# One inversion over nine chunks of a head pair, where two ran over four and five

## The chip, the core and the metric

The program runs on one core of a Trainium2 chip. A core has a matrix engine (PE, whose weight loads are listed as PEld), three elementwise engines (DVE, ACT, POOL) and a queue that issues DMAs (SP). Each engine runs its own list of instructions strictly in the order in which they stand, and waits on semaphores for the others. The metric is the time of one execution on the device in microseconds; the profile is one such execution, taken by the hardware profiler.

## The reference, cut to what matters

Two decoder layers over 512 tokens and 16 learned ones in front (528 in all, width 1024): an RWKV-7 time mixing layer (32 heads of 64), then a latent attention layer. The change lies in the first. Its core is a recurrence over the tokens, one 64x64 state a head:

```python
def step(S, inp):
    r_t, w_t, k_t, v_t, a_t, b_t = inp
    sa = jnp.einsum('bhij,bhj->bhi', S, a_t)
    S = S * w_t[:, :, None, :] + sa[..., None] * b_t[:, :, None, :] + v_t[..., None] * k_t[:, :, None, :]
    return S, jnp.einsum('bhij,bhj->bhi', S, r_t)
```

The term `sa` makes each token depend on all before it in its chunk. Taken 64 tokens at a time, that dependence is a unit triangular 64x64 system for each chunk and head, and its inverse can be made before the state is known.

## The kernel before, in words

Tokens are cut into nine chunks of 64 (the last holds 16). Heads go in pairs, `p` from 0 to 15: one head on partitions 0 to 63, the other on 64 to 127. For each pair the program

- projects k and r (`multiply`: 96 matmuls `pg<-x,w` of 264 columns), and normalises and decays them (`prepare`);
- makes the triangular matrices of the nine chunks (`products`: `M`, in three slices: chunks 0 to 3, 4 to 7, 8);
- inverts them (`inverse`): `Mh` is M in f16, `Mb` and `Qb` are block diagonal forms of it, `Lb` is what f16 lost. Five levels (`lv`) double the size of the inverted blocks. In a level PE multiplies by `Mb`, DVE masks the result into `Xs`, ACT copies `Xs` into a padded tile (`X0`, `X1`, `o`), PE multiplies by `Qb` and ACT writes `Tm`; beside this PE and ACT bring `Qb` up to the next level. A correction step then ends with `Qd`, the inverse that the recurrence reads;
- transposes and scales what the state update needs (`sides`: `KBt`, `SV`);
- runs the recurrence (`recur`, `chunk`): per chunk `pc<-SV,ALR`, evacuated as `xs`; `pc<-xs,Qd`, evacuated into `SV`; `pc<-SV,KBt`, which gives the next state; and two matmuls into `py` for the output. Lane 0 takes chunks 0 to 3 of a pair and lane 1 chunks 4 to 8, so that lane 0 can be in the next pair while lane 1 finishes this one;
- normalises the output (`finish`), and much later gates it (`gate`).

Before, the inversion has two lanes too: `inverse(p, 0)` on chunks 0 to 3 and `inverse(p, 1)` on 4 to 8, each a generator of its own that goes through the pairs in order. `CUT = 4` is the border. The tiles of the inversion exist once each, so a lane starts on the next pair when it is done with this one. `M` exists once, `KB` once, `Qd`, `SV` and `KBt` twice, `ALR` and `MR` three times.

What isn't in this chain fills PE between its steps: the projections of the next pairs, and after pair 15's the 16 units of the gate projection g (48 matmuls each, also `<-x,w`), which nothing needs before the recurrence's end. Then come the output projection (`<-y,w`) and the second layer.

The order of all instructions on all engines is decided while the program is built, by a planner (`Flow`). Each stage is a generator that yields steps; the planner keeps a clock for each engine, takes the step that can start first by its own table of costs, and issues it. A stage named earlier in the list wins if it is within `SLACK` microseconds; the wide matmuls of the projections are put back by `DEFER`; where PE would stand idle and has had little work, it adds a matmul on constants (`pc<-masks`). A projection's result goes to two banks `pg`, or, every other time for some kinds, to `pw`, of which there are four for everything else.

Of the kernel before, what the change touches and what calls it, by code (L numbers as in the profile page):

```python
# [130 lines left out]
class Flow:  # L131
# [9 lines left out]
    SLACK, DEFER = 0.1, 0.1  # L141
# [316 lines left out]
class Layer0:  # L458
# [516 lines left out]
    def invert(self, lane):  # L975

        flow = self.flow
        if lane == 0:
            yield from self.blocks()
            for n in ("Tm", "Mh", "Q"):  # L980
                setattr(self, n, self.tl(1, (128, 9, 64), n, F16))
            for t in (self.Tm, self.Mh, self.Q):
                flow.cut[t.tensor.name] = CUT * 64
            for t in (self.Mb, self.Qb, self.Lb, *self.X):
                flow.cut[t.tensor.name] = CUT * 128
            flow.cut[self.Xs.tensor.name] = CUT * 32
            flow.events.add("blocks")
        yield flow.until("blocks")
# [83 lines left out]
    def inverse(self, p, lane):  # L1072
# [5 lines left out]
        Mb, Qb, Lb, Mh, Tm, Q = (t[:, c0:c1] for t in (self.Mb, self.Qb, self.Lb, self.Mh, self.Tm, self.Q))  # L1078
# [25 lines left out]
        q, v = product(lambda ci: I, Mb)  # L1104
        nc.vector.tensor_tensor(Tm, v, bc(self.mL[0], nn), ALU.mult)
        nc.last(q)
        yield
        for lv in range(1, 6):
            b = 1 << lv
            x = self.Xs[:, c0:c1]  # L1110
            x4 = x.rearrange("p c (g b) -> p c g b", b=b)
            m = half(self.mL[lv], b, 0)
            q, v = product(lambda ci: half(Tm[:, ci, :], b, 0), Mb, n=32)
            nc.vector.tensor_tensor(x4, v.rearrange("p c (g b) -> p c g b", b=b),
                                    m.unsqueeze(1).to_broadcast([128, nn, 32 // b, b]), ALU.mult)
# [6 lines left out]
            q, v = product(lambda ci: x[:, ci, :], Qb, n=32)  # L1122
# [12 lines left out]
        q, v = product(lambda ci: Tm[:, ci, :], Mb, Lb)  # L1135
# [3 lines left out]
        for hs in (H0, H1):  # L1139
            nc.vector.tensor_tensor(Eb[hs, :, hs], bc(self.id16[hs], nn), v[hs], ALU.subtract)  # L1140
        nc.last(q)
        yield
        q, v = product(lambda ci: I, Tb)
        nc.scalar.activation(Q, v, AF.Copy)
        nc.last(q)
# [118 lines left out]
    def stages(self):  # L1264
# [3 lines left out]
        return [self.finish(), self.recur(1), self.recur(0), self.sides(), self.invert(0), self.invert(1), self.within(), self.prepare(), self.tables(), self.norm(),  # L1268
# [932 lines left out]
```

## Time and profile before

| | |
|---|---|
| median of three executions | 1610.45 us (1608.45 to 1613.81) |
| the profiled execution | 1609.79 us, of which the span of its instructions is 1608.0 us |
| PE, DVE, ACT, POOL busy | 1463.8, 1034.9, 942.4, 733.9 us |
| projections of v, lerps, decays | 0 to about 212 us |
| the pairs, from the first inversion to the end of the recurrence | 212.6 to 934.4 us |
| rest of g, output projection of layer 0 | to about 1080 us |
| layer 1 | to 1608 us |

Times in the rows are microseconds from the start of the span, busy times are sums over instructions, and a wait is put down to what came last. A busy PE isn't a PE at its peak: matmuls overlap, and an alone standing small one counts with its whole latency.

### The profile page before, as it was taken

Reading aid. Unit: us, or ns where it says so; the run is one execution under the profiler, and the core shown is the slowest. Engines: PE = TensorE matmul, PEld = TensorE weight load, DVE = VectorE, ACT = ScalarE, POOL = GpSimd, SP = SyncE. Lnnn points to the kernel's source line nnn. Section 1 sums busy time; section 2 is a strip of 40 time slices with the busy share of each in tenths; the row PEclk is TensorE's granted clock in tenths of the full one; section 3 lists DMA queues with packets and bytes.
Section 4 is the critical chain, followed back from the end, with each engine's and each line's share of the span. In section 5 each row is a group of like instructions: output and inputs, shape, how many; then the busy total and the mean of one; then the engine's idle time right before and its main releaser. Section 6 shows DMA issues by size and latency. Waiting matters only on the chain. (4 is left out here: it accounts for less than half of the span.)

```text
span 1608.0 us, 33360 instructions
## 1 busy us (share of the span) xinstructions
PE 1463.8 (91%) x12404; PEld 1301.2 (81%) x12404; DVE 1034.9 (64%) x2304; ACT 942.4 (59%) x2467; POOL 733.9 (46%) x877
## 2 busy tenths in 40 slices
PE   3899988899998998999998999999999999989997
PEld 3898877888887887888887899998778778877786
DVE  7995688787788877778777333035476666656503
ACT  3556655767766667677777674445555545544532
POOL 4453555444544435444445565745523222322654
PEclk7999999999999999999999999999999999999998
DMA  3456622122122122112422257533211111211332
GB/s 113 133 188 223 205 81 74 43 68 68 55 64 66 61 68 68 49 61 88 143 74 82 69 164 253 171 101 93 82 46 48 53 46 54 53 51 45 112 94 84
DMA packets 84690, 148.49 MB, mean 92 GB/s; under 512 B 9392, under 2 KB 18480, under 8 KB 84528
## 3 DMA queue, kind: packets, MB, share of 16 engines
q1 hardware_dynamic: 84528, 146.37, 28.9%
q8 instruction: 97, 1.59, 0.4%
q14 instruction: 65, 0.53, 0.1%
HBM read 112.87 MB, written 33.46 MB: 91 GB/s over the span
## 5 line engine op out<-in xcount | busy, mean ns | idle before, releaser
L322 POOL TENSOR_TENSOR w<-wraw,w 128x512 fp32r<-128x512 f32 (+1 forms) x278 | 371.6, 1343 | 478.8 <-ACT w L322 448.6
L322 PE MATMUL pg<-x,w 128*128 128x264 f32 x2064 | 337.5, 299 | 7.7 <-ACT k L322 3.2
L322 PEld LDWEIGHTS pg<-x,w 128*128 128x128 f32 x2064 | 272.7, 189 | 13.7 <-ACT k L322 5.7
L322 ACT ACTIVATE w<-wraw 128x512 fp32r<-128x512 f32 (+1 forms) x278 | 170.2, 615 | 135.7 <-DMA wraw<-wo 58.5
L322 POOL COPY Sd<-SV 64x64 f32<-64x64 f32 x256 | 73.1, 286 | 187.9 <-DVE SV L322 180.3
L322 PE MATMUL pb<-u,w 128*128 128x512 f32 x384 | 106.2, 405 | 11.9 <-DVE sg L322 11.9
L322 PE MATMUL pg<-lat,w 128*128 128x512 f32 (+1 forms) x480 | 108.5, 367 | 4.9 <-DVE q L322 3.1
L322 PEld LDWEIGHTS pg<-lat,w 128*128 128x128 f32 x480 | 80.6, 197 | 17.4 <-DVE q L322 3.5
L322 PEld LDWEIGHTS pb<-u,w 128*128 128x128 f32 x384 | 68.4, 190 | 25.8 <-DVE sg L322 14.2
L322 PE MATMUL pg<-O,w 128*128 128x512 f32 x336 | 79.1, 395 | 3.2 <-ACT acc L322 1.5
L322 PEld LDWEIGHTS pg<-O,w 128*128 128x128 f32 x336 | 62.9, 188 | 19.1 <-ACT acc L322 1.9
L322 DVE SCALAR_TENSOR_TENSOR SV<-Sd,PC,pc 64x64 f32<-64x64 f32 x224 | 59.8, 279 | 22.3 <-PE pc L322 17.5
L322 PE MATMUL pc<-xs,Qd 128*128 128x64 f32 x288 | 54.4, 286 | 20.4 <-ACT xs L322 19.0
L322 PEld LDWEIGHTS <-Mb 128*128 128x128 f16 x1152 | 59.0, 98 | 16.4 <-issue 6.4
L322 POOL TENSOR_TENSOR Lb<-M,Mh 64x256 f16<-64x256 f32 (+1 forms) x64 | 50.4, 787 | 42.8 <-ACT Mh L322 38.8
L322 PEld LDWEIGHTS pc<-xs,Qd 128*128 128x128 f32 x288 | 41.4, 189 | 34.3 <-ACT xs L322 29.8
L322 PE MATMUL pc<-SV,KBt 128*128 128x128 f32 x256 | 54.2, 312 | 9.5 <-DVE SV L322 7.6
L322 DVE SCALAR_TENSOR_TENSOR sg<-sg,par,rs 128x264 f32<-128x264 f32 x32 | 16.0, 532 | 71.9 <-ACT rs L322 71.9
L322 DVE TENSOR_TENSOR Xs<-pw,masks 128x128 f16<-128x128 f32 (+1 forms) x160 | 47.7, 301 | 21.4 <-PE pw L322 9.6
L322 DVE COPY SV<-pc 64x64 f32<-64x64 f32 x176 | 36.3, 225 | 38.4 <-ACT SV L322 32.7
L322 PE MATMUL pw<-Tm,Mb 128*128 128x32 f16 (+1 forms) x864 | 54.7, 180 | 4.8 <-ACT Tm L322 3.8
L322 PE MATMUL pc<-SV,ALR 128*128 128x128 f32 x288 | 57.2, 286 | 1.1 <-ACT xs L322 0.5
(375 smaller groups left out, 3906.7 us busy)
## 6 DMA issues: line engine op xcount, KB each, us to landing
wraw<-wr SPq DMA_DIRECT2D x120, 256.0 KB, 2.9
wraw<-wo SPq DMA_DIRECT2D x64, 256.0 KB, 2.7
wraw<-wi SPq DMA_DIRECT2D x46, 256.0 KB, 2.7
d_v<-gx SPq DMA_DIRECT2D x16, 264.0 KB, 3.0
d_c<-o SPq DMA_DIRECT2D x16, 264.0 KB, 2.4
c<-d_c SPq DMA_DIRECT2D x16, 264.0 KB, 3.0
a<-d_a SPq DMA_DIRECT2D x16, 264.0 KB, 3.1
vx<-d_v SPq DMA_DIRECT2D x16, 264.0 KB, 2.9
```

The costliest lines, as they stand in the source:

```text
L322: getattr(eng, method)(*args, **kw)
```

## The change

`inverse` works on all nine chunks at once, and one generator goes through the pairs. An elementwise operation that stood twice (4 and 5 chunks) stands once over nine; where a product has 64 columns a chunk, nine don't fit a PSUM bank (576 over 512), so it takes two banks, and its evacuation stays two instructions. The inversion of a pair starts on the event that all nine chunks' `M` are there (`("M", p, True)`). The last evacuation into `Qd` keeps its two parts and two waits. `SLACK` goes from 0.1 to 0.12, `DEFER` from 0.1 to 0.05.

```diff
-    SLACK, DEFER = 0.1, 0.1
+    SLACK, DEFER = 0.12, 0.05
...
-    def invert(self, lane):
+    def invert(self):
...
         for p in range(NP):
-            yield flow.until(("M", p, lane == 1))
-            yield from self.inverse(p, lane)
+            yield flow.until(("M", p, True))
+            yield from self.inverse(p)
...
-        c0, c1 = ((0, CUT), (CUT, 9))[lane]
-        nn = c1 - c0
-        M = self.st[p]["M"][:, c0:c1]
+        nn = 9
+        M = self.st[p]["M"]
...
         def product(rhs, *lhs, n=64):
 
-            q = self.one()
-            qv = q[:, 0 : nn * n].rearrange("p (c t) -> p c t", t=n)
-            for ci in range(nn):
-                for i, l in enumerate(lhs):
-                    nc.tensor.matmul(qv[:, ci, :], l[:, ci, :], rhs(ci), start=(i == 0), stop=(i == len(lhs) - 1))
-            return q, qv
+            out = []
+            for cs in ((0, CUT), (CUT, 9)) if n == 64 else ((0, 9),):
+                q = self.one()
+                qv = q[:, 0 : (cs[1] - cs[0]) * n].rearrange("p (c t) -> p c t", t=n)
+                for ci in range(*cs):
+                    for i, l in enumerate(lhs):
+                        w = l[:, ci, :]
+                        nc.tensor.matmul(qv[:, ci - cs[0], :], w, rhs(ci), start=(i == 0), stop=(i == len(lhs) - 1))
+                out.append((q, qv, slice(*cs)))
+            return out
...
-        q, v = product(lambda ci: Q[:, ci, :], Eb)
-        for hs in (H0, H1):
-            nc.vector.scalar_tensor_tensor(Qd[hs, c0:c1, hs], v[hs], -1.0, Q[hs], ALU.mult, ALU.subtract)
-        nc.last(q)
-        nc.event(("within", p, lane))
-        yield
+        for lane, (q, v, cs) in enumerate(product(lambda ci: Q[:, ci, :], Eb)):
+            if lane and p >= 2:
+                yield self.flow.until(("recur", p - 2))
+            for hs in (H0, H1):
+                nc.vector.scalar_tensor_tensor(Qd[hs, cs, hs], v[hs], -1.0, Q[hs, cs], ALU.mult, ALU.subtract)
+            nc.last(q)
+            nc.event(("within", p, lane))
+            yield
...
-        return [self.finish(), self.recur(1), self.recur(0), self.sides(), self.invert(0), self.invert(1), self.within(), self.prepare(), self.tables(), self.norm(),
+        return [self.finish(), self.recur(1), self.recur(0), self.sides(), self.invert(), self.within(), self.prepare(), self.tables(), self.norm(),
```

Counted over the whole program, PE keeps its matmuls but for the idle-time ones (`pc<-masks`: 8 before, 37 now). ACT loses 256 instructions: `Mh` 32 to 16, `X0`/`X1`/`o` 256 to 128, `Tm` 160 to 80, `Mb<-Tm` 64 to 32. DVE loses 144: `Mb` and `Qb` 64 to 32 each, `Xs` 160 to 80. POOL loses 32 (`Lb`). Five units of g move from `pw` to `pg`, since `early` in `gemm` asks whether pair 15's inversion has been issued.

On DVE, around the end of pair 7's inversion. Before (`M_1389` and `ALR_1370` are pair 8's, `Qd_834` is pair 7's, `Xs` is lane 0 of pair 8, and the last row starts lane 1 of pair 8):

```order
L322 TENSOR_TENSOR M_1389_7834<-pw_1410_8000,masks_235 64x64
L322 TENSOR_TENSOR MR_1388_7833<-pw_1410_8000,masks_235 128x64
L322 TENSOR_TENSOR ALR_1370_7700<-pw_1410_8000,masks_235 64x64
L322 TENSOR_TENSOR M_1389_7834<-pw_1411_8001,masks_235 64x64
L322 TENSOR_TENSOR MR_1388_7833<-pw_1411_8001,masks_235 128x64
L322 COPY xs1_1413_8021<-pc_181_348 64x64
L322 TENSOR_TENSOR ALR_1370_7700<-pw_1411_8001,masks_235 64x64
L322 SCALAR_TENSOR_TENSOR Qd_834_3625<-pw_1416_8041,Q_668_2467 64x5x64 x2
L322 TENSOR_TENSOR sq_650_2404<-k_1343_7503,sq_650_2404 128x528
L322 COPY xs0_1419_8092<-pc_181_348 64x64
L322 TENSOR_TENSOR Xs_2450<-pw_1425_8112,masks_235 128x128
L322 TENSOR_TENSOR Mb_1385<-Mh_667_2466,masks_235 64x5x64
```

Lane 1 starts on pair 8 right behind its end on pair 7, with pair 8's last `M` just made, and lane 0 is by then in its levels. Now (`ALR_1304` ends pair 8's products, `Qd_864` is pair 7's, the last row starts pair 8's inversion, `xs0` is the first chunk of pair 7 and `xs1` a late chunk of pair 6):

```order
L322 TENSOR_TENSOR ALR_1304_7484<-pw_1329_7686,masks_235 64x64
L322 TENSOR_TENSOR Qb_1393<-masks_235,pw_1332_7703 64x5x64 x2
L322 TENSOR_TENSOR sq_650_2401<-k_1237_6927,sq_650_2401 128x528
L322 COPY SV_1191_6579<-pc_181_348 64x64
L322 SCALAR_TENSOR_TENSOR Qd_864_3949<-pw_1339_7793,Q_667_2466 64x4x64 x2
L322 SCALAR_TENSOR_TENSOR SV_1191_6579<-Sd2_661_2453,PC_1115_5950,pc_181_348 64x64 x2
L322 COPY xs0_1343_7818<-pc_181_348 64x64
L322 SCALAR_TENSOR_TENSOR Qd_864_3949<-pw_1340_7794,Q_667_2466 64x5x64
L322 SCALAR_TENSOR_TENSOR inv_651_2402<-k_1237_6927,par_58,inv_651_2402 128x528
L322 COPY xs1_1344_7840<-pc_181_348 64x64
L322 SCALAR_TENSOR_TENSOR Qd_864_3949<-pw_1340_7794,Q_667_2466 64x5x64
L322 TENSOR_TENSOR Mb_1387<-Mh_666_2465,masks_235 64x9x64
```

Pair 8's `M` is made before pair 7's inversion ends, and pair 8's inversion follows that end at once; no other inversion runs beside it. Pair 7's chunk 0 stands behind its `Qd`, with lane 1 of pair 6 nearly done.

On ACT, in the levels of pair 8's inversions. Before (4x and 5x are lanes 0 and 1):

```order
L322 ACTIVATE Tm_666_2465<-pw_1434_8193 128x16x8
L322 ACTIVATE Qb_1390<-pw_1437_8208 128x32x8
L322 ACTIVATE o_656_2411<-Xs_2450 64x4x2x16 x2
L322 ACTIVATE X0_653_2408<-Xs_2450 64x5x16x2 x2
L322 ACTIVATE Y_1288_7085<-py_182_349 64x128
L322 ACTIVATE Tm_666_2465<-pw_1440_8241 128x8x16
L322 ACTIVATE Qb_1390<-pw_1442_8266 128x16x16
L322 ACTIVATE Tm_666_2465<-pw_1441_8252 128x80x2
L322 ACTIVATE Y_1288_7085<-py_182_349 64x128
L322 ACTIVATE Qb_1390<-pw_1444_8278 128x160x2
L322 ACTIVATE Tm_666_2465<-pw_1445_8285 128x4x32
```

The two lanes' copies stand in one another's gaps. Now (9x; the level's two `Qb` halves are two instructions):

```order
L322 ACTIVATE X0_653_2405<-Xs_2450 64x9x16x2
L322 ACTIVATE Tm_665_2464<-pw_1368_8012 128x144x2
L322 ACTIVATE xs0_1367_8009<-pc_181_348 64x64
L322 ACTIVATE Qb_1393<-pw_1369_8024 128x128x2
L322 ACTIVATE Qb_1393<-pw_1370_8025 128x160x2
L322 ACTIVATE SV_1278_7323<-pc_181_348 64x64
L322 ACTIVATE w_1372_8059<-wraw_1341_7814 128x512
L322 ACTIVATE X1_654_2406<-Xs_2450 64x9x8x4 x2
L322 ACTIVATE Tm_665_2464<-pw_1376_8081 128x72x4
L322 ACTIVATE Qb_1393<-pw_1377_8099 128x64x4
L322 ACTIVATE Qb_1393<-pw_1378_8100 128x80x4
L322 ACTIVATE xs0_1374_8062<-pc_181_348 64x64
```

A level is X, X, Tm, Qb, Qb, with a step of the recurrence and one projection weight (`w`) between two levels.

On PE, at the recurrence's last matmuls (`py`). Before:

```order
L322 MATMUL pw_13866<-x_11925,w_13758 128x264
L322 MATMUL py_349<-ALR_12599,Sd_662_2454 128x32
L322 MATMUL py_349<-MR_12703,SV_13124 128x32
L322 MATMUL pw_13867<-x_11925,w_13757 128x264
L322 MATMUL pw_13867<-x_11926,w_13757 128x264
L322 MATMUL pw_13867<-x_11925,w_13758 128x264
```

Behind them stand 381 matmuls of g. Now:

```order
L322 MATMUL pg_13589<-x_11245,w_13541 128x264
L322 MATMUL py_349<-ALR_12044,Sd_662_2454 128x32
L322 MATMUL py_349<-MR_12190,SV_12570 128x32
L322 MATMUL pg_13701<-x_11090,w_13586 128x264
L322 MATMUL pg_13701<-x_11091,w_13586 128x264
L322 MATMUL pg_13701<-x_11090,w_13587 128x264
```

Behind them stand 144; the other 237 have moved in front. Layer 1 has the same instructions in a partly different order, since `SLACK` holds there too.

## Rows read from the trace of the kernel before

**Rows 1.** The page's first part: busy us, share of the span and instructions.

```profile
PE 1463.8 (91%) x12404; PEld 1301.2 (81%) x12404; DVE 1034.9 (64%) x2304; ACT 942.4 (59%) x2467; POOL 733.9 (46%) x877
```

**Rows 2.** Engines by stretch: us, PE, PEld, DVE, ACT, POOL busy (instructions), clock, DMA, GB/s.

```profile
212.60:388.50 175.90, 158.04 (x1762) 139.72 (x1760) 146.60 (x380) 116.71 (x358) 83.33 (x129) 0.98 0.19 61
388.50:854.40 465.90, 425.92 (x4790) 379.19 (x4788) 367.68 (x1009) 325.03 (x1002) 215.70 (x355) 1.00 0.22 72
854.40:934.60 80.20, 75.61 (x727) 69.62 (x725) 37.90 (x123) 57.72 (x167) 44.03 (x64) 1.00 0.29 87
```

**Rows 3.** Timeline, ACT: start, us, instruction; where pair 6's and 7's inversions start.

```profile
456.35 0.42 ACT L322 ACTIVATE Mh<-M 128x256 f16<-128x256 f32 x1
...
470.36 0.46 ACT L322 ACTIVATE Mh<-M 128x320 f16<-128x320 f32 x1
...
512.89 0.46 ACT L322 ACTIVATE Mh<-M 128x320 f16<-128x320 f32 x1
```

**Rows 4.** Timeline, DVE: where the two inversions of pair 6 end.

```profile
490.98 0.43 DVE L322 SCALAR_TENSOR_TENSOR Qd<-pw,Q 64x256 f32<-64x256 f32 x1
...
511.02 0.49 DVE L322 SCALAR_TENSOR_TENSOR Qd<-pw,Q 64x320 f32<-64x320 f32 x1
```

**Rows 5.** Timeline, ACT: the first inversion of five chunks starts.

```profile
223.02 0.45 ACT L322 ACTIVATE Mh<-M 128x320 f16<-128x320 f32 x1
```

**Rows 6.** Instructions on tile Mh: count, ns min/median/max, first and last start.

```profile
L322 ACT ACTIVATE Mh<-M x32: 399/436/471, 212.6 to 861.6; 128x256 f16<-128x256 f32 x16, 128x320 f16<-128x320 f32 x16
```

**Rows 7.** Groups by shape, whole span: count, busy us, mean ns, idle before and releasers.

```profile
L322 PE MATMUL pw<-Xs,Qb 128*128 128x32 f16 x720 | 42.3, 177 | 4.9 <-DVE Xs L322 4.8
...
L322 DVE TENSOR_TENSOR Xs<-pw,masks 128x160 f16<-128x160 f32 x80 | 25.3, 316 | 6.5 <-PE pw L322 5.0 <-ACT Y L322 0.6 <-issue 0.2
...
L322 ACT ACTIVATE Tm<-pw 128x160 f16<-128x160 f32 x80 | 23.8, 297 | 11.1 <-PE pw L322 10.1
...
L322 DVE TENSOR_TENSOR Xs<-pw,masks 128x128 f16<-128x128 f32 x80 | 22.9, 287 | 14.9 <-PE pw L322 4.7 <-ACT Qb L322 4.1 <-ACT X L322 1.7
...
L322 ACT ACTIVATE Tm<-pw 128x128 f16<-128x128 f32 x80 | 21.8, 272 | 7.8 <-PE pw L322 6.4
...
L322 ACT ACTIVATE X<-Xs 64x160 f16<-64x160 f16 x64 | 21.3, 332 | 5.2 <-DVE Xs L322 4.1
...
L322 ACT ACTIVATE X<-Xs 64x128 f16<-64x128 f16 x64 | 19.5, 305 | 13.9 <-DVE Xs L322 13.1
...
L322 DVE TENSOR_TENSOR Mb<-Mh,masks 64x320 f16<-64x320 f16 x32 | 18.8, 588 | 2.7 <-ACT Mh L322 2.2
...
L322 DVE TENSOR_TENSOR Mb<-Mh,masks 64x256 f16<-64x256 f16 x32 | 15.3, 478 | 0.9 <-ACT Mh L322 0.3
...
L322 DVE SCALAR_TENSOR_TENSOR Qd<-pw,Q 64x256 f32<-64x256 f32 x32 | 13.5, 420 | 1.7 <-PE pw L322 0.7 <-ACT Qb L322 0.5
...
L322 ACT ACTIVATE Mb<-Tm 64x256 f16<-64x256 f16 x32 | 13.2, 412 | 1.7 <-PE pw L322 1.3
```

**Rows 8.** Timeline, PE: one product of a level on five chunks.

```profile
479.63 0.28 PE L322 MATMUL pw<-Xs,Qb 128*128 128x32 f16 x5
```

**Rows 9.** Instructions on tile xs, DVE, window 245 to 277 us (pair 0).

```profile
L322 DVE COPY xs<-pc x5: 208/217/217, 245.7 to 276.5; 64x64 f32<-64x64 f32 x5
```

**Rows 10.** The same, window 910 to 932 us (pair 15, last five chunks).

```profile
L322 DVE COPY xs<-pc x5: 216/217/217, 911.0 to 929.2; 64x64 f32<-64x64 f32 x5
```

**Rows 11.** Timeline, ACT: the last piece of the recurrence's output leaves PSUM.

```profile
934.26 0.18 ACT L322 ACTIVATE Y<-py 64x16 f32<-64x16 f32 x1
```

**Rows 12.** Timeline, PE: two units of the gate projection, back to back.

```profile
938.36 6.02 PE L322 MATMUL pg<-x,w 128*128 128x264 f32 x48
944.22 6.01 PE L322 MATMUL pw<-x,w 128*128 128x264 f32 x48
```

**Rows 13.** Timeline, ACT: a unit's two halves leave their banks.

```profile
955.75 0.76 ACT L322 ACTIVATE inv<-pg 128x264 f32<-128x264 f32 x2 [0.54 <-PE pg L322]
```

**Rows 14.** Instructions on tile masks, PE: the idle-time matmuls.

```profile
L322 PE MATMUL pc<-masks x8: 269/273/283, 210.9 to 701.2; 128*128 128x256 f16 x8
```

More of the change, by code (lines that the diff above doesn't have):

```diff
@@ L973, in blocks @@
         yield
-    def invert(self, lane):
+    def invert(self):
         flow = self.flow
[L978 to L988, printed above, removed]
+        yield from self.blocks()
+        for n in ("Tm", "Mh", "Q"):
+            setattr(self, n, self.tl(1, (128, 9, 64), n, F16))
+        for t in (self.Tm, self.Mh, self.Q):
+            flow.cut[t.tensor.name] = 9 * 64
+        for t in (self.Mb, self.Qb, self.Lb, *self.X):
+            flow.cut[t.tensor.name] = 9 * 128
+        flow.cut[self.Xs.tensor.name] = 9 * 32
         for p in range(NP):
-            yield flow.until(("M", p, lane == 1))
-            yield from self.inverse(p, lane)
+            yield flow.until(("M", p, True))
+            yield from self.inverse(p)
     def products(self, p):
@@ L1070, in side, with inverse @@
         yield
-    def inverse(self, p, lane):
+    def inverse(self, p):
         nc = self.nc
-        c0, c1 = ((0, CUT), (CUT, 9))[lane]
-        nn = c1 - c0
-        M = self.st[p]["M"][:, c0:c1]
-        Mb, Qb, Lb, Mh, Tm, Q = (t[:, c0:c1] for t in (self.Mb, self.Qb, self.Lb, self.Mh, self.Tm, self.Q))
+        nn = 9
+        M = self.st[p]["M"]
+        Mb, Qb, Lb, Mh, Tm, Q = self.Mb, self.Qb, self.Lb, self.Mh, self.Tm, self.Q
         nc.scalar.activation(Mh, M, AF.Copy)
@@ L1103, in inverse @@
         I = self.id16
-        q, v = product(lambda ci: I, Mb)
-        nc.vector.tensor_tensor(Tm, v, bc(self.mL[0], nn), ALU.mult)
-        nc.last(q)
+        for q, v, cs in product(lambda ci: I, Mb):
+            nc.vector.tensor_tensor(Tm[:, cs], v, bc(self.mL[0], cs.stop - cs.start), ALU.mult)
+            nc.last(q)
         yield
+        x = self.Xs
         for lv in range(1, 6):
             b = 1 << lv
-            x = self.Xs[:, c0:c1]
             x4 = x.rearrange("p c (g b) -> p c g b", b=b)
             m = half(self.mL[lv], b, 0)
-            q, v = product(lambda ci: half(Tm[:, ci, :], b, 0), Mb, n=32)
+            (q, v, _), = product(lambda ci: half(Tm[:, ci, :], b, 0), Mb, n=32)
             nc.vector.tensor_tensor(x4, v.rearrange("p c (g b) -> p c g b", b=b),
@@ L1121, in inverse @@
             yield
-            q, v = product(lambda ci: x[:, ci, :], Qb, n=32)
+            (q, v, _), = product(lambda ci: x[:, ci, :], Qb, n=32)
             nc.scalar.activation(half(flat(Tm), b, 0), v.rearrange("p c (g b) -> p (c g) b", b=b), AF.Copy)
@@ L1127, in inverse @@
             yield
-            q, v = product(lambda ci: half(Qb[:, ci, :], b, 1), X)
-            nc.scalar.activation(half(flat(Qb), b, 1), v.rearrange("p c (g b) -> p (c g) b", b=b), AF.Copy)
-            nc.last(q)
-            yield
+            for q, v, cs in product(lambda ci: half(Qb[:, ci, :], b, 1), X):
+                nc.scalar.activation(half(flat(Qb[:, cs]), b, 1), v.rearrange("p c (g b) -> p (c g) b", b=b), AF.Copy)
+                nc.last(q)
+                yield
         yield
         Eb, Tb = Qb, Mb
-        q, v = product(lambda ci: Tm[:, ci, :], Mb, Lb)
+        out = product(lambda ci: Tm[:, ci, :], Mb, Lb)
         yield
@@ L1138, in inverse @@
             nc.scalar.activation(Tb[hs, :, hs], Tm[hs], AF.Copy)
-        for hs in (H0, H1):
[L1140 to L1145, printed above, removed]
+        for q, v, cs in out:
+            for hs in (H0, H1):
+                nc.vector.tensor_tensor(Eb[hs, cs, hs], bc(self.id16[hs], cs.stop - cs.start), v[hs], ALU.subtract)
+            nc.last(q)
+            yield
+        for q, v, cs in product(lambda ci: I, Tb):
+            nc.scalar.activation(Q[:, cs], v, AF.Copy)
+            nc.last(q)
         yield
         if p >= 2:
-            yield self.flow.until(("recur", p - 2) if lane else ("chunk", p - 2, CUT - 1))
+            yield self.flow.until(("chunk", p - 2, CUT - 1))
         if p == 1:
             yield self.flow.until(("v", NP - 1))
-        if p < 2 and p == len(self.Qd):
+        if p < 2:
             t = self.tl(2, (128, 9, 128), "Qd")
```

8 lines of the change are left out of this document (4 added, 4 removed).

## The prediction

> **What bounds the kernel now.** I read the busy times first, then the engines by stretch, then the timeline around the inversions, and last the groups by shape.
>
> The busy times [rows 1] call PE the bound at 91%, but the stretches [rows 2] show that this share hides two regimes. In the pairs (212.6 to 934.4 us) PE shows 91% in the middle stretch, with DVE at 79% and ACT at 70%. Many of PE's instructions there are small f16 matmuls that count with their latency: one of 32 columns shows 177 ns [rows 7], though five in a row take only 0.28 us [rows 8]. So PE isn't full there; it is held by chains that go PE, elementwise engine, PE. Behind the pairs g runs dense: 48 matmuls from 938.36 to 944.22 us, 0.122 us each [rows 12].
>
> Which chain? Lane 1 of the inversion starts pair 6 at 470.36 us and ends it at 511.51; it starts pair 7 at 512.89 [rows 3, 4]. That is 41.2 us of work and 1.4 us to the next pair: the lane has no slack. From its first start, 223.02 us [rows 5], to the last, 861.6 [rows 6], lie 15 pairs: 42.6 us a pair. Lane 0 needs 35.0 us for pair 6 (456.35 to 491.41) and stands idle for the rest. So a pair costs 42.6 us, and a lane of inversion is one of the chains that set it. The recurrence is close: with one lane and no inversion its chunks follow every 4.55 us (911.0 to 929.2, four steps) [rows 10]; beside two inversions every 7.7 us (245.7 to 276.5, four steps) [rows 9].
>
> **What the change removes.** 256 ACT and 144 DVE instructions. The two shapes give the fixed part: `X` takes 305 ns on 128 elements and 332 on 160, so 0.84 ns an element and 197 ns fixed; `Tm` likewise 172 ns, `Xs` 171 [rows 7]. ACT: 128 x 0.197 + 80 x 0.172 + 48 x 0.2 = 48.6 us, 3.0 a pair. DVE: 80 x 0.171 and little for `Mb` (its fixed part is 38 ns) and `Qb`, 15 to 20 us, 1 a pair. None of this lies on PE, and neither engine is full, so by itself it is worth nothing; it counts only as shorter waits.
>
> The Trainium skill (Perfetto Trace Analysis, Optimizing Scalar/DVE Operations) gives about 93 ns of overhead for a Scalar instruction from SBUF and 51 from PSUM; by that the ACT saving would be an estimate of 176 x 0.093 + 80 x 0.051 = 20 us. The rows show more than twice that, and the rows decide.
>
> **What it adds: one chain in place of two.** The order shows that pair p+1's `M` is made before pair p's inversion ends, and that p+1's inversion follows at once. So, if the chip follows it, the pairs go at the length L of a merged inversion, and everything turns on L. No row shows it. Two ways to bound it.
>
> First, work and waits. One lane of four chunks by its own operations [rows 3, 7, 8]: Mh 0.42, two Mb 0.96, PE 0.28, Tm on DVE about 0.42 (taken like Qd); five levels of PE 0.26, Xs 0.29, two X 0.61 (PE's product by Qb beside them), Tm 0.27, 7.15 together; then PE 0.39, Mb<-Tm 0.82, PE 0.28, Q about 0.41 (taken like Mb<-Tm), PE 0.28, two Qd 0.84. Sum 12.2 us. With five chunks 13.7, so 1.5 a chunk; nine give 19.7, and about 0.5 for evacuations that stay two, 20.2 us. Measured were 35.0 and 41.2, so 22.8 and 27.5 us were waits for engines busy with other things. If all of lane 1's waits stay, L is 47.7. The other lane's own 13 us in 42.6, about a third, is what leaves the queues of two of the three engines; taking waits down by two thirds of a third gives 20.2 + 17.9 = 38.1 by lane 0 and 20.2 + 21.6 = 41.8 by lane 1, in the middle 40. From below, PE's share of 91% in 42.35 us (465.9 us in 11 pairs) [rows 2] is 38.7 us, and that work stays.
>
> Second, recurrence steps. In the new order seven chunk steps stand between one pair's `Qd` and the next's, with one recurrence lane at work for most of it and one inversion beside it. A step lies between 4.55 and 7.7 us [rows 9, 10], in the middle 6.1: L = 43, with ends 32 and 54.
>
> I take 41.4, between 40 and 43, and keep 38.7 and 47.7 as ends.
>
> **The sum.** The first merged inversion waits for all nine `M`, as lane 1 did: 223.0 us. Sixteen end at 223.0 + 16 x 41.4 = 885.4. Pair 15's nine chunks then run with one lane at work and no inversion beside: 9 x 4.55 = 41 and some for the output pieces, 45: the recurrence ends at 930.4, against 934.4 [rows 11]: -4.
>
> Behind that end stand 237 fewer matmuls of g. They run dense there, at 5.86 us for 48 [rows 12], so -28.9 us. They are hidden in front if PE has room: from pair 15's preparation on it has one inversion and then one recurrence lane, both made of waits. What covers them is this waiting; if it weren't there they would cost the 28.9 again (a rival below).
>
> Costs: five more units of g in `pg` alone have to wait until the unit before has left its two banks, 0.76 us [rows 13] less what runs beside, 3 us in all. The 29 more idle-time matmuls take 0.27 us each [rows 14], 8 us, in time that is idle by the planner's clock; a quarter of it counted, 2. Layer 1's other order I count at nothing; its instructions are the same; it may give or take 6. After the recurrence, `finish` and the gate of pair 15 had 46 us of g to hide behind and now have 18; the gate needs its own g unit, the last, anyway, so nothing is late.
>
> -4 - 28.9 + 5 = -28, so 1609.8 - 28 = 1582 for an execution like the profiled one. The median of the runs shown is 0.7 above the profiled one, so I stay at 1582.
>
> The time moves by 16 us for each microsecond of L: 1539 at 38.7, 1683 at 47.7, and no change at 43.15.
>
> **The rivals.**
>
> *A single chain has nothing to fill its waits (slower).* Before, while lane 0 waited for ACT, lane 1 used PE; a wait on either hit half the chunks. Now every wait of every hop is on the only path, and each operation on it is longer: by the slopes above X grows to 0.44 us and Tm to 0.40, and Qb has two evacuations in a row; and each `xs` of the recurrence that falls behind an X waits 0.44 instead of 0.31. And each pair's recurrence starts only at its `Qd`, with the lane before it all but done, so that its two lanes hardly overlap. It decides from L = 43.15 on, which is only 1.75 over my value. For it: lane 1's waits of 27.5 us are as likely as lane 0's. Against it: ACT and DVE lose 3 and 1 us a pair. At L = 45: 223 + 720 + 45 = 988, +53.6 - 28.9 + 5, so 1639.
>
> The Trainium skill says in the same section that where Scalar and Vector aren't saturated but make other engines wait, breaking instructions up may let work end sooner. That speaks against this change; the rows do show unsaturated engines, ACT 70% and DVE 79%, and whether the merged pieces make PE wait longer no run here shows yet. By it the time would be this rival's.
>
> *The moved g work isn't hidden (no change).* If PE's queue delays the last pairs by all of the 237 matmuls, the 28.9 us come back: 1609.8 - 4 + 5 = 1611. For it: PE is shown 94% busy in 854 to 934 us [rows 2]. Against: the same stretch holds small matmuls with their latencies.
>
> *The waits shrink far more (much faster).* If half of lane 0's waits go, L would be 31.6, but PE's 38.7 stops it. Between 38.7 and 40.3: 1539 to 1565. For it: lane 0 ended pair 6 in 35.0 with lane 1 in its way.
>
> *The chip doesn't follow the order's pace.* If pair p+1's `M` comes late, as lane 1's did (1.4 us), period 42.6: 223 + 681.6 + 45 = 949.6, +15.2 - 28.9 + 5, so 1601. It lies in the forecast's own range.
>
> **How the numbers follow.** A measurement of this kernel tells 0.3%, about 5 us, from no change. Forecast (L from 40.3 to 42.8, 1565 to 1605): 0.45. Slower (L from 43.5 on): 0.26. No change (hidden work comes back, or L at 43): 0.12. Much faster: 0.17. So faster 0.62, same 0.12, slower 0.26. The range leaves out the far ends: L from 39.2 to 44.7, which is 1547 to 1635. The forecast's own range is 1565 to 1605.
>
> **What would show it.** In the changed profile: 16 `Mh` of 576 elements, each within 1.5 us of the last `Qd` of the pair before, and L as their distance, 41.4, below 43.15 for a gain. `X` of 9 chunks at 0.44, `Tm` at 0.40. Chunk steps of 5 to 6.5 us in the middle pairs, with `xs0` of a pair less than 2 us behind its first `Qd`. The last `Y` at about 930 us, and about 18 us of g behind it. The granted clock at 0.98 to 1.00 in the pairs, as now [rows 2]. Layer 1's length within 6 us of 528. I am wrong if `Mh` comes at 43 us or more, if it waits for `M` instead of for `Qd`, if g behind the end is short but the end itself lies 25 us later, or if layer 1 moves by more than 6.

## The result and the profile after

The change makes the kernel slower: 1658.16 us (1654.61 to 1661.99, four runs) against 1609.45 beside it, a ratio of 1.0304 [1.0274, 1.0333]. 1582 was forecast, with 1547 to 1635 as the range. The profiled execution took 1657.63 us, its span is 1655.8, so 47.8 more than before.

The first part of the page, as in [rows 1]:

```profile
PE 1485.1 (90%) x12433; PEld 1315.8 (79%) x12433; DVE 1036.3 (63%) x2160; ACT 905.4 (55%) x2211; POOL 729.4 (44%) x845
```

ACT fell by 37.0 us. PE rose by 21.3, and the span less PE's busy time, its idle time, from 144.2 to 170.7 us: those two are the loss. (A busy time counts a moment in which two instructions of an engine overlap once; it is not the sum over instructions that the section on the profile before calls it. Added up one by one, ACT's instructions fell from 1046.8 to 999.4 us, by 47.4, and DVE's from 1109.7 to 1085.4, by 24.3.)

By stretch, columns as in [rows 2]: pair 4's inversion start to pair 15's, pair 15, and the g work behind.

```profile
395.20:905.50 510.30, 458.50 (x4987) 408.33 (x4986) 380.00 (x947) 313.59 (x865) 224.75 (x346) 0.95 0.21 70
905.50:998.80 93.30, 87.14 (x808) 80.76 (x809) 47.07 (x110) 66.53 (x172) 52.89 (x70) 1.00 0.35 113
998.80:1017.30 18.50, 16.33 (x124) 15.36 (x123) 6.10 (x8) 12.22 (x23) 10.44 (x8) 1.00 0.67 211
```

Eleven pairs take 510.3 us, with PE at 90% and the clock at 0.95. Before, lane 1 started on the same two pairs at 387.8 and 861.6 us, 473.8 apart (the 465.9 of [rows 2] run from about the end of one pair's inversion to that of the eleventh after it). The rows where an inversion starts and the one before it ends answer to [rows 3, 4], from the timelines of ACT and DVE:

```profile
538.75 0.68 ACT L322 ACTIVATE Mh<-M 128x576 f16<-128x576 f32 x1
...
586.96 0.68 ACT L322 ACTIVATE Mh<-M 128x576 f16<-128x576 f32 x1
```

```profile
586.72 0.49 DVE L322 SCALAR_TENSOR_TENSOR Qd<-pw,Q 64x320 f32<-64x320 f32 x1
```

and the tile's row to [rows 6]:

```profile
L322 ACT ACTIVATE Mh<-M x16: 667/683/686, 219.6 to 905.5; 128x576 f16<-128x576 f32 x16
```

Pair 7 starts at 538.75 and ends at 587.21; pair 8 starts at 586.96, beside that last instruction. From the first start to the last lie 15 pairs of 45.7 us (42.6 before).

Groups by shape, columns as in [rows 7]:

```profile
L322 PE MATMUL pc<-xs,Qd 128*128 128x64 f32 x288 | 59.9, 299 | 28.4 <-ACT xs L322 26.7
L322 PE MATMUL pc<-SV,KBt 128*128 128x128 f32 x256 | 59.6, 319 | 20.9 <-DVE SV L322 19.6 <-DVE xs L322 0.4
...
L322 DVE TENSOR_TENSOR Xs<-pw,masks 128x288 f16<-128x288 f32 x80 | 36.4, 454 | 11.6 <-PE pw L322 5.3 <-ACT ysq L322 3.0 <-ACT Qb L322 1.1
...
L322 ACT ACTIVATE Tm<-pw 128x288 f16<-128x288 f32 x80 | 32.5, 406 | 12.3 <-PE pw L322 11.4
...
L322 PE MATMUL pw<-Xs,Qb 128*128 128x32 f16 x720 | 31.1, 178 | 4.2 <-DVE Xs L322 4.0
...
L322 ACT ACTIVATE xs<-pc 64x64 f32<-64x64 f32 x144 | 29.7, 216 | 97.6 <-DVE xs L322 90.5 <-PE py L322 2.4 <-DVE SV L322 1.3
...
L322 ACT ACTIVATE X<-Xs 64x288 f16<-64x288 f16 x64 | 28.1, 439 | 11.4 <-DVE Xs L322 10.6
```

and those three of before that [rows 7] didn't show:

```profile
L322 PE MATMUL pc<-xs,Qd 128*128 128x64 f32 x288 | 54.4, 286 | 20.4 <-ACT xs L322 19.0 <-DVE SV L322 0.3 <-DVE Tm L322 0.2
L322 PE MATMUL pc<-SV,KBt 128*128 128x128 f32 x256 | 54.2, 312 | 9.5 <-DVE SV L322 7.6 <-DVE xs L322 0.4 <-ACT gx L322 0.3
...
L322 ACT ACTIVATE xs<-pc 64x64 f32<-64x64 f32 x144 | 28.8, 216 | 45.4 <-DVE xs L322 38.6 <-DVE SV L322 3.5 <-PE pc L322 1.4
```

The merged pieces have the sizes that were forecast (`X` 0.44, `Tm` 0.41), and PE's products by `Qb` even fell from 42.3 us to 31.1. The growth shows in the recurrence's rows: ACT idles 97.6 us ahead of its `xs` where it idled 45.4, PE 28.4 ahead of `pc<-xs,Qd` (20.4) and 20.9 ahead of `pc<-SV,KBt` (9.5). These two hold 19.4 of the 26.5 us that PE idles more.

The last output piece, on ACT's timeline, and the last unit of g on PE's answer to [rows 11, 12]:

```profile
998.53 0.18 ACT L322 ACTIVATE Y<-py 64x16 f32<-64x16 f32 x1
```

```profile
1011.12 6.12 PE L322 MATMUL pg<-x,w 128*128 128x264 f32 x48 [1.71 <-ACT sq L322]
```

So the recurrence ends 64.3 us later (998.7 for 934.4), g behind it takes 18.5 us in place of 45.1 (the last unit ends at 1017.3; before, at 979.5), and what follows 638.5 in place of 628.5: +64.3 - 26.6 + 10.0 = +47.7.

The 10.0 lie in layer 1, from the last matmul `<-y,w` to the end. Its row before, in the changed kernel, and in the run below that changes `SLACK` alone:

```profile
1080.10:1608.00 527.90, 487.74 (x2719) 406.46 (x2717) 283.07 (x572) 250.68 (x559) 204.46 (x170) 0.98 0.23 67
```

```profile
1117.80:1655.80 538.00, 491.11 (x2718) 409.05 (x2717) 281.62 (x572) 250.27 (x558) 204.11 (x170) 0.97 0.22 65
```

```profile
1118.30:1662.20 543.90, 492.73 (x2718) 411.24 (x2717) 282.69 (x572) 250.48 (x558) 204.21 (x170) 0.97 0.22 64
```

### The profile page after: what moved, and what is told of

Its sections match the earlier page's. It is cut to its first block, busy times and chain, and to the rows that moved or that the text cites. A ratio compares the mean times of both kernels' runs of the same rounds, so it can differ in the third digit from the quotient of the medians.

```text
span 1655.8 us, 32909 instructions
## 1 busy us (share of the span) xinstructions
PE 1485.1 (90%) x12433; PEld 1315.8 (79%) x12433; DVE 1036.3 (63%) x2160; ACT 905.4 (55%) x2211; POOL 729.4 (44%) x845
## 4 chain that ended last, share of the span: by engine, by line
PE 39%; DVE 13%; ACT 12%; issue 3%; POOL 2%; DMA 0%; ACTq 0%; DVEq 0%; POOLq 0%; SPq 0%
PE pg L322 17%; PE pw L322 5%; PE pc L322 5%; PE pb L322 4%; PE py L322 3%; PE pd L322 2%; DVE sg L322 2%; PE ps L322 2%; DVE SV L322 1%; DVE qr L322 1%; ACT w L322 1%; ACT gx L322 1%; DVE mx L322 1%; PE pe L322 1%; ACT ysq L322 1%
## 5 line engine op out<-in xcount | busy, mean ns | idle before, releaser
L322 POOL TENSOR_TENSOR w<-wraw,w 128x512 fp32r<-128x512 f32 (+1 forms) x278 | 366.9, 1326 | 465.3 <-ACT w L322 437.6
L322 PE MATMUL pg<-x,w 128*128 128x264 f32 x2304 | 370.3, 299 | 7.2 <-ACT r L322 2.7
L322 PEld LDWEIGHTS pg<-x,w 128*128 128x128 f32 x2304 | 304.9, 191 | 14.4 <-ACT r L322 3.9
L322 PEld LDWEIGHTS pg<-lat,w 128*128 128x128 f32 x480 | 80.7, 197 | 23.3 <-DVE q L322 10.4
L322 PEld LDWEIGHTS pb<-u,w 128*128 128x128 f32 x384 | 69.7, 193 | 24.1 <-DVE sg L322 12.2
L322 PE MATMUL pc<-xs,Qd 128*128 128x64 f32 x288 | 59.9, 299 | 28.4 <-ACT xs L322 26.7
L322 PEld LDWEIGHTS pc<-xs,Qd 128*128 128x128 f32 x288 | 44.0, 195 | 49.8 <-ACT xs L322 42.6
L322 ACT ACTIVATE xs<-pc 64x64 f32<-64x64 f32 x144 | 29.7, 216 | 97.6 <-DVE xs L322 90.5
L322 DVE SCALAR_TENSOR_TENSOR SV<-Sd,PC,pc 64x64 f32<-64x64 f32 x224 | 62.6, 279 | 28.4 <-PE pc L322 21.1
L322 PE MATMUL pc<-SV,KBt 128*128 128x128 f32 x256 | 59.6, 319 | 20.9 <-DVE SV L322 19.6
L322 PEld LDWEIGHTS pc<-SV,KBt 128*128 128x128 f32 x256 | 40.1, 196 | 33.0 <-DVE SV L322 29.3
L322 ACT ACTIVATE Y<-py 64x128 f32<-64x128 f32 (+1 forms) x160 | 40.0, 250 | 44.8 <-PE py L322 43.2
L322 PE MATMUL pc<-SV,ALR 128*128 128x128 f32 x288 | 61.8, 301 | 0.3
L322 PE MATMUL pw<-ALR,KB 64*128 64x128 f32 x576 | 53.8, 319 | 5.7 <-DVE ALR L322 5.3
```

Source lines behind the costliest of these rows:

```text
L322: getattr(eng, method)(*args, **kw)
```

## The experiments

All ran beside the kernel before; a ratio is to it, and a period is the mean distance from one pair's inversion start to the next's. Those on the changed kernel come first, then those on the kernel before, then the ones that fit both.

**Constants of before on the changed kernel.**

```diff
-    SLACK, DEFER = 0.12, 0.05
+    SLACK, DEFER = 0.1, 0.1
```

> The changed kernel with the planner's two constants of the kernel before (SLACK 0.1 and DEFER 0.1 in place of 0.12 and 0.05). Theory A, the single chain and its waits set the pairs' period: the constants are not the cause, the time stays between 1650 and 1668 us and the period of a pair (Mh to Mh) at 45.5 to 46.5 us. Theory C, the constants let the wide matmuls of g go before the small ones of the chain: most of the loss goes, 1610 to 1630 us and a period of 43 to 44.

1676.88 us, 1.0422 [1.0402, 1.0442]: slower still. Neither theory has this; the two constants are worth 19 us to the changed kernel, with the sign against theory C. So the merge alone, with the constants of before, costs 68.9 us, more than merge and constants together.

**A level less.** The kernel leaves out the last of the five doublings (also where two other lines ask for the last level), so its result isn't the inverse.

```diff
-        for lv in range(1, 6):
+        for lv in range(1, 5):
```

> The changed kernel with the last of the five levels of the inversion left out (the result is not the inverse; its work per pair is one Xs, one Tm, two X, one Qb and their matmuls less). Theory A, the chain of the inversion sets the period: one level is 6.1 us of 46.0 in the trace of the changed kernel, so the period falls to 40 to 41 us, and the time by 16 x 5 to 6 us, to 1560 to 1580. Theory F, the recurrence (49 to 53 us from a pair's first Qd to its end, its two lanes hardly overlapped) sets the period: the period falls by under 1.5 us and the time stays above 1635.

1640.26 us, 1.0188 [1.0165, 1.0211], a period of 44.5. The inversion of a pair is 5.6 us shorter (mean of pairs 3 to 14) and the period 1.2. Where the rest went, on the timelines of DVE and ACT (start, us):

```profile
648.76 0.49 DVE L322 SCALAR_TENSOR_TENSOR Qd<-pw,Q 64x320 f32<-64x320 f32 x1
...
664.28 0.21 DVE L322 TENSOR_TENSOR M<-pw,masks 64x64 f32<-64x64 f32 x1
...
665.50 0.23 DVE L322 TENSOR_TENSOR M<-pw,masks 64x64 f32<-64x64 f32 x1
```

```profile
665.93 0.67 ACT L322 ACTIVATE Mh<-M 128x576 f16<-128x576 f32 x1
```

Pair 9's inversion ends at 649.25, but pair 10's M is finished only at 665.73, and `Mh` follows at once. M stands at the end of another chain (projection, preparation, products) on the same engines. In 9 of the 15 pairs `Mh` comes more than 1.5 us behind the end of the pair before. So the inversion isn't alone in setting the period, which the forecast took it to be. Theory F, the recurrence, has both numbers right; but the row in front of `Mh` is `M`, and the recurrence's own length isn't fixed either (from a pair's first chunk to its last, mean of pairs 1 to 14, 49.0 us in the changed kernel and 42.8 in a run with fitted constants below).

**One lane after the other.**

```diff
-            yield flow.until(("M", p, lane == 1))
+            yield flow.until(("M", p, lane == 1), *([("within", p, 0)] if lane else [("within", p - 1, 1)] if p else []))
```

(An event that `M` has been read was added too, so that the next pair's `M` is written behind it.)

> The kernel before with its two lanes of inversion one after the other: lane 1 of a pair waits for the end of lane 0, lane 0 of the next pair for the end of lane 1; all instructions as before, four and five chunks each. It is the loss of concurrency without the merge. Theory A: two chains of hops in a row, 12.2 + 13.7 us of own work and some 20 us of waits each, so a period of 60 to 66 us and 1870 to 1990 us; the merge then is worth 14 to 20 us a pair, and the missing second chain costs more than that. Theory E, the longer merged instructions and what they block are the cause and concurrency is worth little: a period of 43 to 48 us and 1610 to 1690 us.

1759.04 us, 1.0944 [1.0926, 1.0962], 56.1 us from lane 1's start on a pair to its start on the next. It lies between the theories. Against this one order, running the two lanes beside each other gains 13.5 us a pair (42.6), merging them 10.4 (45.7).

**Three lanes of three chunks.** (`M` comes in slices of three chunks too, and the recurrence's lane 0 waits for two of the three inversions.)

```diff
-        c0, c1 = ((0, CUT), (CUT, 9))[lane]
+        c0, c1 = ((0, 3), (3, 6), (6, 9))[lane]
```

> The kernel before with three lanes of inversion of three chunks each (M made in slices of three chunks too) in place of four and five. More instructions: by the fixed parts of Xs, X, Tm and Mb about 3 us of ACT and 1 us of DVE more a pair. Theory A, a chain's waits are filled by other chains: the period (42.6 us) falls to 39.5 to 42, the time to 1560 to 1600 us. A rival, that the instructions' fixed parts and the queues they fill decide: period 43.5 to 46 and 1625 to 1665 us. Theory F, the recurrence sets the period: 1600 to 1620.

1662.84 us, 1.0343 [1.032, 1.0366]: more chains are not faster, against theory A, at least in this order. The rival that fixed parts and queues decide has the time; ACT's busy time rose by 36.8 us, to 979.2.

**More and no warm matmuls.**

```diff
-    GAP, FED = 0.15, 3400
+    GAP, FED = 0.12, 4200
```

> The changed kernel with the planner's rule for warm matmuls made more generous (GAP 0.12 and FED 4200 in place of 0.15 and 3400): 141 matmuls of masks in idle time in place of 37. Between 210 and 1130 us the trace of the changed kernel has 79 us at half clock, the kernel before 14, and PE's exclusive busy time is 28 us longer there than at full clock, before 4. Theory B, the half clock is a cause of its own worth about 24 us: the stretches at half clock fall under 40 us and the time to 1635 to 1652. Against it, the half clock only shows that PE idles and its slower matmuls lie in waits: the stretches fall and the time stays at 1653 to 1675 us, the added matmuls paid.

and with `GAP, FED = 0.15, 0`:

> The changed kernel without any warm matmul (FED 0): none of masks in idle time in place of 37. Theory B, the half clock is a cause of its own: the stretches at half clock grow from 79 us to over 100 and the time to 1665 to 1690 us. Against it: the stretches grow and the time stays within 1645 to 1662 us.

1654.57 us, 1.0272 [1.0242, 1.0303], and 1659.76, 1.032 [1.0301, 1.0338]. The windows from the first `Mh` to the end of the recurrence, with the most warm matmuls and with none:

```profile
219.50:1001.40 781.90, 707.07 (x7612) 631.39 (x7609) 564.60 (x1359) 485.78 (x1306) 364.02 (x530) 0.97 0.22 73
```

```profile
220.00:997.00 777.00, 702.84 (x7423) 629.71 (x7423) 560.11 (x1357) 482.59 (x1297) 356.00 (x530) 0.94 0.21 71
```

The clock moved (0.97 and 0.94; 0.95 for the changed kernel over the same stretch) and the time hardly did. Between 200 and 1130 us the changed kernel has 79 us at half clock; with 104 matmuls more they shrank only to 65 us, not under 40, and without any they grew to 106. As a cause of its own worth some 24 us the half clock falls, as far as these two runs move it.

**Lanes in step.**

```diff
-            yield flow.until(("M", p, lane == 1))
+            yield flow.until(("M", p, True))
+            if p:
+                yield flow.until(("within", p - 1, 0), ("within", p - 1, 1))
```

> The kernel before with its two lanes of inversion kept in step: both start a pair when all of M is there and both lanes have ended the pair before. All instructions as before, two chains, but both halves of Qd come at about one time, as in the changed kernel. Theory G, it is the number of chains beside each other that decides, the recurrence's two lanes among them: the recurrence from a pair's first chunk to its last shrinks from 65 us to 48 to 55 (no overlap of its lanes with the next pair's), PE idles 8 to 20 us more, the period is 43.5 to 45.5 us and the time 1630 to 1655. Theory A, one chain of inversion instead of two: two chains are left, so a period of 42 to 43 and 1605 to 1622 us. Theory E, the longer merged instructions: 1605 to 1622 us too.

1658.47 us, 1.0309 [1.0287, 1.0331]: the loss of the change, to the microsecond, with no instruction merged. But the recurrence still takes 65.6 us from a pair's first chunk to its last (mean of pairs 1 to 14; before 66.6, the changed kernel 49.0), so theory G, whose range ends 3 us below, doesn't have the mechanism. A and E forecast no loss here; that one comes without the merge doesn't show yet that the merge costs none.

**X behind Tm.**

```diff
-                    nc.scalar.activation(X[...], x4[hs], AF.Copy)
             yield
             (q, v, _), = product(lambda ci: x[:, ci, :], Qb, n=32)
             nc.scalar.activation(half(flat(Tm), b, 0), ...)
...
             yield
+            for hs in (H0, H1):
+                nc.scalar.activation(X[...], x4[hs], AF.Copy)
```

> The changed kernel with the two X copies of a level (0.44 us each on ACT) noted behind the Tm of that level, so that Tm doesn't stand behind them in ACT's queue. Theory A, the length of the chain sets the period: a level is 0.5 to 0.9 us shorter, four of them a pair, so the period falls by 2 to 3.5 us to 42.5 to 44 and the time to 1605 to 1628 us. Theory G (fewer chains leave PE idle and at half clock, and PE's work with its waits sets the period, as the run without a level suggests, in which a chain shorter by 5 us gave 1.2 us of period): 1645 to 1665 us.

1659.38 us, 1.0317 [1.0299, 1.0334], period 45.6: the shorter hop is worth nothing.

By now every variant, whatever it did, had come out at 1640 to 1677, or slower. That suggested theory T: the order of the kernel before is a fitted one, and most others cost 2 to 3%. The next three runs change the order of the kernel before, with its two lanes left alone.

**Only SLACK.**

```diff
-    SLACK, DEFER = 0.1, 0.1
+    SLACK, DEFER = 0.12, 0.1
```

> The kernel before, two lanes and all, with SLACK 0.12 in place of 0.1 and nothing else: another order of the same instructions. So far every variant, merged or not, in step or in three lanes, came out at 1640 to 1663 us. Theory T, the order of the kernel before is one fitted to its shape by its constants, and most other orders of the same work cost some 2 to 3%, whatever the change: 1640 to 1670 us, with 40 to 90 us at half clock. Theories A and G (one chain in place of two, the merge itself, or the recurrence's lanes): the two lanes are still there, 1600 to 1622 us.

**Only the start wait.**

```diff
-            yield flow.until(("M", p, lane == 1))
+            yield flow.until(("M", p, True))
```

> The kernel before with lane 0 waiting for all nine M, as the merged inversion does, and nothing else; the lanes are free of each other afterwards. Theory T: another order, 1630 to 1660 us. Theory D, the start wait alone is a part of the loss: 1.4 us a pair at most by lane 1's wait in [rows 3, 4], so 1610 to 1632 us. Theories A and G: 1605 to 1620 us.

**Both constants of the change, no merge.**

```diff
-    SLACK, DEFER = 0.1, 0.1
+    SLACK, DEFER = 0.12, 0.05
```

(The event that `M` has been read is in this run too, as in the lanes one after the other.)

> The kernel before with both constants of the change (SLACK 0.12, DEFER 0.05) and without the merge; M of a pair is also not written before both lanes have read the pair before (an event that keeps the order free of a deadlock). Theory T: 1635 to 1665 us, so that the merge adds nothing to what the constants cost. Theory A: 1605 to 1622 us, and the merge is the whole loss.

1664.93 us, 1.0357 [1.033, 1.0383]; 1644.1, 1.0229 [1.0203, 1.0255]; 1665.84, 1.0361 [1.0334, 1.0388]. Theory T each time, the last 0.8 us above its range. The last is the control that matters: the constants alone cost what the whole change costs, and more. With the merge alone (68.9 us) the three don't add up: 56.9 for the constants, 68.9 for the merge, 48.7 for both. No part of the loss can be put down to one of the two lines of the change; what they share is that each makes another order. The first parts of the pages of the first and the last:

```profile
PE 1492.7 (90%) x12427; PEld 1319.8 (79%) x12427; DVE 1038.1 (62%) x2304; ACT 939.3 (57%) x2467; POOL 725.6 (44%) x877
```

```profile
PE 1486.1 (89%) x12423; PEld 1315.9 (79%) x12423; DVE 1049.4 (63%) x2304; ACT 940.7 (57%) x2467; POOL 731.2 (44%) x877
```

Same instructions as before but for 23 and 19 warm matmuls and, behind pair 15's inversion, three and five units of g that go to other banks; PE is busy 28.9 and 22.3 us more and idle 25.3 and 30.9 more (spans 1662.2 and 1661.2), the picture of the changed kernel.

**The changed kernel with constants fitted to it.**

```diff
-    SLACK, DEFER = 0.12, 0.05
+    SLACK, DEFER = 0.13, 0.125
```

> The changed kernel with the two constants fitted anew to the merged chain (SLACK 0.13, DEFER 0.125 in place of 0.12 and 0.05): one chain still, 12 warm matmuls in place of 37. Theory T: most of the loss is the order's and comes back, 1610 to 1635 us, a period of 42.5 to 44.5 us and under 40 us at half clock. Theory A, the single chain costs: 1645 to 1665 us and a period of 45 to 46.5.

1606.75 us, 0.9987 [0.9968, 1.0005]: the whole loss is back, with every hop of the merged chain still there, and more of it than T's 1610 to 1635. The period is 41.4 us, the L of the forecast (`Mh` from 217.4 to 839.0 us). (Fitted means: values whose order ends early by the planner's own clock, at 1524 to 1540 us in the four fitted runs.)

**A hundredth.**

```diff
-    SLACK, DEFER = 0.1, 0.1
+    SLACK, DEFER = 0.099, 0.1
```

> The kernel before with SLACK 0.099 in place of 0.1 and nothing else: a hundredth of the constant, the same instructions in another order. Theory T, the order decides and the kernel before is one fitted order among many that cost 2 to 4% more: 1630 to 1665 us. Theory C in its plain form, the constants act by their size (a larger SLACK or a smaller DEFER is worse): a change of a hundredth does nothing, 1605 to 1614 us.

1636.88 us, 1.0168 [1.0142, 1.0195], on the kernel before. In the pairs the constants don't act by their size; a change of a hundredth gives another order, and that costs 1.7%.

**Two more fits of the changed kernel, one of the kernel before.**

```diff
-    SLACK, DEFER = 0.12, 0.05
-    AHEAD, SPARE = 0.25, 0.35
+    SLACK, DEFER = 0.134, 0.103
+    AHEAD, SPARE = 0.25, 0.6
```

> The changed kernel, one chain, with constants fitted to it over four of them (SLACK 0.134, DEFER 0.103, AHEAD 0.25, SPARE 0.6); 5 warm matmuls. Theory T, and the forecast's mechanism where the order fits (period 40 to 42 us as in t4_fit, but with more of g in front of the recurrence's end): 1585 to 1605 us. Theory A, the single chain costs in itself, and t4_fit was the best it can do: 1606 us or more.

1619.16 us, 1.0057 [1.0036, 1.0079]; a miss for T's 1585 to 1605. And with `SLACK, DEFER = 0.13, 0.079` and `AHEAD, SPARE = 0.15, 0.2`:

> As the run before, the changed kernel with other fitted constants (SLACK 0.13, DEFER 0.079, AHEAD 0.15, SPARE 0.2); 7 warm matmuls. Theory T: 1585 to 1610 us, period 40 to 42.5. Theory A: 1606 us or more.

1598.24 us, 0.9925 [0.9901, 0.9949]: 0.75% less than the kernel before, with a single chain. The kernel before with `DEFER` 0.095:

> The kernel before, two lanes, with DEFER 0.095 in place of 0.1, the constants that fit it best near its own: the fair comparison for a merged chain with fitted constants. Theory T: the kernel before is already at its own best, 1598 to 1614 us. A rival, that any kernel of this kind gains 1% from a renewed fit: 1590 to 1598 us.

1603.1 us, 0.9952 [0.9936, 0.9968]. The two intervals overlap: between these two fitted orders the merge is worth between 0.7% gained and 0.1% lost.

That whole hides two parts. Up to the end of g the two fitted merged orders at 1607 and 1598 us are ahead, at 960.2 and 954.2 us, where the fitted two lanes are at 970.8. Layer 1 then takes them 543.4 and 544.6 us for 526.0, and that goes with `SLACK`: in the eight kernels with 0.1 or 0.099 layer 1 takes 523.7 to 530.0 us, in the ten with 0.12 to 0.134 536.7 to 544.6, merged or not. A merged order with layer 1 at 526.0 would come to some 1585 to 1589 us, an estimate from these rows; no run has it.

What a fitted order looks like, in the run at 1598 us (the execution traced took 1603.15): eleven pairs by window, starts of four inversions on ACT's timeline, and three groups by shape.

```profile
381.50:835.50 454.00, 436.56 (x4922) 388.30 (x4920) 377.09 (x952) 314.53 (x859) 232.29 (x347) 1.00 0.24 78
```

```profile
502.77 0.67 ACT L322 ACTIVATE Mh<-M 128x576 f16<-128x576 f32 x1
...
543.14 0.67 ACT L322 ACTIVATE Mh<-M 128x576 f16<-128x576 f32 x1
...
583.67 0.67 ACT L322 ACTIVATE Mh<-M 128x576 f16<-128x576 f32 x1
...
624.02 0.67 ACT L322 ACTIVATE Mh<-M 128x576 f16<-128x576 f32 x1
```

```profile
L322 PE MATMUL pc<-xs,Qd 128*128 128x64 f32 x288 | 61.7, 296 | 11.5 <-ACT xs L322 9.8
L322 PE MATMUL pc<-SV,KBt 128*128 128x128 f32 x256 | 59.5, 314 | 9.2 <-DVE SV L322 7.8 <-DVE xs L322 0.2
...
L322 ACT ACTIVATE xs<-pc 64x64 f32<-64x64 f32 x144 | 31.3, 218 | 66.5 <-DVE xs L322 61.2 <-DVE SV L322 1.9 <-PE py L322 1.5
```

The same instructions as in the changed kernel but for 30 warm matmuls (37 there, 7 here) and three units of g that go to other banks. Nine pairs in a row follow every 40.4 to 40.5 us, one like the other; the eleven take 454.0 us in place of 510.3, PE is at 96% in them in place of 90, the clock at 1.00. ACT's idle time ahead of `xs` is 66.5 us in place of 97.6, PE's ahead of `pc<-xs,Qd` 11.5 in place of 28.4.

What stays open is why the planner, from nearly the same constants, settles into such a rhythm in one order and not in another. That orders with a rhythm wait less is seen; that the rhythm is what makes them wait less was not tested.

## Why the prediction was wrong

The step that failed is "I take 41.4", the length of a merged inversion as a number that the merge has. Sixteen took 45.7 us each, 68.1 us more than forecast in all. The rest of the sum stood within 5 us a term: the first started 3.4 earlier, pair 15's chunks took 48.6 in place of 45, g behind gave 26.6 in place of 28.9, and what follows cost 10.0 in place of 5. Together that is 1582 + 75.6 = 1657.6, the execution that was profiled. The rival of the single chain, priced at L = 45, gave 1639 and its side. But the rival's reason falls as well: in the fitted run at 1598 us nothing else inverts beside the merged chain either, and it goes at 41.0 us a pair.

Why 41.4 couldn't be had from the rows: the waits (22.8 and 27.5 us by lane) were taken for a property of a chain and split between sources. The runs show that they belong to the order in which the chains are laid into the engines' queues. The same work came out at 1603 to 1666 us on two lanes (the run with one lane behind the other left out) and at 1598 to 1677 on one (the run with a level less left out). The constants in the first line of the diff make such another order, and no term, bound or rival of the prediction prices them: on two lanes they cost 56.9 us (1665.84 for 1608.91, with the event on M's reading; `SLACK` alone, with nothing else, 56.0). Yet with them at their old values the forecast wouldn't have come out either: the merge alone, in the order that they give it, costs 68.9.

The prediction says that no row shows L. The planner had a number for it. By its own clock, which is a calculation in the program and not a measurement, the merged inversions end 44.4 us apart (pairs 3 to 15), where the two lanes' ended 42.1 and 40.9 apart, and the last instruction ends at 1563 us in place of 1527: three quarters of the loss. The fitted orders end at 1524 to 1540 by that clock, and the slower ones with all five levels at 1557 and later. So the loss is in the order as planned, for the most part, and not in the chip falling behind it. (A slip in the first bound changes little: the fifth level has no X, so the own work of the lanes is 0.6 to 0.7 us less than the 12.2 and 13.7 of the prediction, and the waits as much more.)

A second, smaller step: "Layer 1's other order I count at nothing". It took 10.1 us more, and by the run with `SLACK` alone, 16.0 more on unmerged lanes, that is the price of `SLACK`.

Point by point:

- *ACT 48.6 us less, DVE 15 to 20*: right for ACT as a sum over instructions, which it was (47.4), and a little low for DVE (24.3); as busy time, ACT 37.0 less and DVE 1.4 more. The shorter waits that this was to give are not to be seen. The Trainium skill (Perfetto Trace Analysis, Optimizing Scalar/DVE Operations) calls its overheads engine-busy times and puts the latency in a profile at about twice that; so for durations as the rows show them the estimate by that page is about 40 us, not 20. The trace's 47.4 is nearer to that.
- *`Mh` within 1.5 us of the last `Qd`*: so in 14 of 15 pairs; in pair 5 it waited 3.0 us for M. Right.
- *Chunk steps of 5 to 6.5 us, `xs0` within 2 us of `Qd`*: 6.6 on lane 0, 5.8 on lane 1 (pairs 1 to 14); 0 to 2.7 behind. Right but for a little at the upper ends. As a bound for L they were circular: in that fitted run they are 6.3 and 4.6, shorter with the period.
- *L alone sets the period*: wrong. A level less took 5.6 us from L and 1.2 from the period, as M came late next.
- *237 matmuls of g hidden in front, 18 us of g behind*: 18.5. That they were hidden there isn't shown; they lie in the stretch that grew.
- *Costs of 5 us, layer 1 within 6*: layer 1 took 10.1 us more. Missed by 4, a sign of being wrong that the prediction had named itself.
- *Clock 0.98 to 1.00*: 0.95. Wrong, though the runs with more and with no warm matmuls speak against it as the main cause.
- *The Trainium skill's rule* (the same section) that broken-up instructions may let work end sooner gave the right sign. The runs don't show its reason at work: the same instructions, unmerged, lose as much with these constants, and merged ones with fitted constants lose nothing.

## What to carry to other kernels

Where a planner writes the order, its constants are a part of the change. Read the planner's own end time first: here it had most of the loss. Price a diff of constants with a control that has them alone and one that has the rest alone, and compare two shapes only when both have been fitted, stretch by stretch: constants that fit one part can cost another, as `SLACK` does layer 1. Before believing a few per cent, move one constant by a hundredth and see how far the time goes: here 1.7%. And a chain's waits, averaged in one order, don't go along with its instructions into another.

## What the hardware showed unasked

A run of nine small matmuls covers less of PE's time than runs of four and five: the 720 products `Xs,Qb` cover 31.1 us for 42.3 [rows 7], while each still shows 177 or 178 ns. An estimate from [rows 7, 8] gives both: five in a row take 0.28 us, so each behind the first adds some 0.026, and 80 runs of nine come to 31 us, 80 of four and 80 of five to 43. What the run saves is the first one's latency, once a run. Whether PE did other work in that time isn't shown.

And matmuls added to keep the clock up bought nothing that the time shows: 104 of them raised the mean clock of the pairs from 0.95 to 0.97 and PE's busy time there by 4.5 us (702.6 to 707.1), and the kernel took 3.6 us less, inside the spread of either kernel's runs.
